# A hybrid decoder layer on one core: a new order for its mixing stage, products k by k between the stages, and both ends rewritten

## The chip, the cores and the metric

The kernel runs on one core of a Trainium2 chip. The metric is the device time of one execution in microseconds (us), the median of the runs shown. TensorE (PE) does the matmuls, VectorE (DVE), ScalarE (ACT) and GpSimd (POOL) the elementwise work, SyncE (SP) issues most of the transfers; each engine works through its own queue in order.

## The reference

512 tokens of 1024 channels in float32 go through a feed-forward layer, a mixing layer of two head groups, and a second feed-forward layer. Each of the three is normed ahead of and behind, and added to x:

```python
def reference(x, ...):
    h = rms_norm(x, ffn1_pre_g)
    x = x + 0.5 * rms_norm(swiglu(h, ffn1_w_in, ffn1_w_out), ffn1_post_g)
    h = rms_norm(x, mix_pre_g)
    q, k, v, u = split(h @ w_mix_in)            # 4 x 512 columns
    attn = dilated_attention(q, k, v)           # 8 heads of 64, causal, with a linear bias
    ssm = s5_mixer(u, ...)                      # 32 groups of 16 channels, 64 complex states each
    mixed = concat([attn, ssm]) @ w_mix_out
    x = x + rms_norm(mixed, mix_post_g)
    h = rms_norm(x, ffn2_pre_g)
    return x + 0.5 * rms_norm(swiglu(h, ffn2_w_in, ffn2_w_out), ffn2_post_g)
```

swiglu is silu(h W1) * (h W2) through 2816 hidden channels. s5_mixer runs a linear recurrence over the tokens, adds a skip term to its output, takes gelu of the sum y, and returns y * sigmoid(y w_glu + b_glu).

## The kernel before

Activations lie with channels on the 128 partitions and tokens along the free axis: a tile holds 8 slices k of 128 channels and 512 tokens. Every operand of a product is split into a high part in a reduced float format and a low part that holds the rest, and `mm3` (L123) multiplies high by high, high by low and low by high into one PSUM bank; so a product over 8 slices is 24 matmuls. A weight is loaded to a tile wraw (3 buffers), ACT casts it to whi and DVE or POOL subtracts for wlo (4 buffers each); `load` (L97) does all of that, and `load_tail` (L104) the same into tiles tw that hold the weights of a product's last slices.

`start` loads x and the first weights in pieces, with SP issuing all transfers, among them smalls (gains and the first weight slice, into sw); PE does six warm-up products idle<-warm meanwhile, and then the products first over k = 0 to 7. `ffn` does the first feed-forward layer; its fill work computes the parameters of the state-space model (`ssm_params`, on DVE, ACT and POOL, two of its tiles being gb and cz). `boundary` stands between two stages: it finishes the last product of the stage behind (yt), norms and adds (`prep`, with a DVE product, sum and low part xl and an ACT high part xh for each k), and begins the products first of the next stage (`begin`), in two halves of 256 tokens, h = 0 and 1. The small products st sum squares over partitions, and rp spreads the result back.

`mix` is the mixing stage. Products prj make q and k, prv makes v; U, the input of the recurrence, is written out (ud<-uT) and read back in another layout (um<-ud). The products st<-um make the states of 128 blocks of four tokens, and `scan` then combines the blocks on DVE in a row of short units; `go(n)` records n units of it, `f(n)` n pieces of the products prj and prv, so the code writes out by hand how these interleave. A pair of heads goes through scores (sc), biased maximum (DVE), exponential (ACT), scaling, transposes (pt, copied to ptt), values (pv) and cat, of which ACT writes the high and DVE the low part. Then come ys (the output of the recurrence, with loads w2<-w2d), gelu (tiles ge, zg, zz), gl (the gate), and mo, the output product, whose first four slices come from cat and whose last four are left to the boundary as a tail. The last stage is a feed-forward layer that ends in `finish`: the last product yt by tokens, a sum with y (gather), squares with a sum on ACT, the gain and the final scaling, and the output's transfer, for four blocks b of 128 tokens in two halves d of 512 channels; DVE's order there is written out.

Matmuls, and every instruction passed through `fix`, keep the order in which the program records them on their engine. All others are placed by the scheduler of the tile framework, which moves them ahead or behind by its own estimates and the buffers.

## Time and profile before

| | us |
|---|---|
| runs | 975.64, 972.04, 975.0 |
| median | 975.0 |
| the profiled execution | 973.89 |
| its span, first to last instruction | 972.1 |

The mean granted clock of PE over the span is 0.99 of full speed. The table gives times of whole executions; the rows further down come from the profiled one, with times from the start of its span. The span's stages are: start and first layer to about 378 us, the first boundary to 406, the mixing stage to about 560, the second boundary, and the last layer.

### The profile page before, as it was taken

What the parts mean: (1) busy time and instruction counts of PE and PEld (TensorE: products, weight loads), DVE (VectorE), ACT (ScalarE), POOL (GpSimd) and SP (SyncE); (2) the same over time, 40 slices, a digit from 0 to 9 for tenths busy, and PEclk for the clock granted to TensorE, in tenths of its full rate; (3) what the DMA queues carried; (4) which work ended last, traced back from release to release, by engine and by line L of the source; (5) the groups of instructions that cost most, each with busy time, mean ns of one, the idle gap of its engine ahead of it and who ended that gap; (6) DMA issues with size and microseconds to landing.
All of it is one profiled execution on the core that took longest, in us unless ns stands there. A gap on an engine that the chain in (4) does not pass through costs nothing.

```text
span 972.1 us, 12842 instructions
## 1 busy us (share of the span) xinstructions
PE 949.6 (98%) x5072; PEld 793.7 (82%) x5072; DVE 528.9 (54%) x930; ACT 370.9 (38%) x612; POOL 223.3 (23%) x134
## 2 busy tenths in 40 slices
PE   9999999999999999999998899999999999999996
PEld 7888888888888899888766699888888888888885
DVE  7997214553266437667978458554225433544427
ACT  7353324442233234455474444443333222323312
POOL 2322212322143133400010024422122212222300
PEclk9999999999999999999998899999999999999998
DMA  7233334353334240482323420322222322333202
GB/s 255 94 109 114 100 112 142 99 188 103 109 109 136 58 152 24 114 217 87 121 75 97 143 87 2 109 87 87 87 95 101 108 87 87 108 103 128 94 1 87
DMA packets 38029, 102.48 MB, mean 105 GB/s; under 512 B 7600, under 2 KB 10672, under 8 KB 37424
## 3 DMA queue, kind: packets, MB, share of 16 engines
q1 hardware_dynamic: 37104, 98.50, 31.7%
q10 hardware_dynamic: 864, 3.15, 0.9%
q8 instruction: 40, 0.66, 0.3%
q14 instruction: 21, 0.17, 0.1%
HBM read 94.03 MB, written 7.60 MB: 105 GB/s over the span
## 4 chain that ended last, share of the span: by engine, by line
PE 88%; DVE 6%; ACT 2%; DMA 2%; issue 1%; SPq 0%; POOL 0%; DVEq 0%; POOLq 0%; ACTq 0%
PE gu L120 46%; PE yo L120 20%; PE yt L120 6%; PE first L120 3%; PE prj L120 3%; PE prv L120 2%; PE mo L120 1%; PE st L120 1%; PE gl L120 1%; DVE xl L143 1%; DVE x L302 1%; PE pv L120 1%; PE pt L819 1%; DVE Hs L1085 1%; DMA wraw<-wmot 1%
## 5 line engine op out<-in xcount | busy, mean ns | idle before, releaser
L93 ACT CAST whi<-wraw 128x1024 fp32r<-128x1024 f32 (+5 forms) x157 | 155.3, 991 | 314.5 <-PE gu L120 129.2
L95 POOL TENSOR_TENSOR wlo<-wraw,whi 128x1024 fp32r<-128x1024 f32 (+2 forms) x62 | 155.9, 2515 | 519.3 <-ACT whi L93 519.3
L120 PE MATMUL gu<-xh,whi 128*128 128x512 f32 x656 | 257.6, 393 | 0.0
L120 PE MATMUL gu<-xh,wlo 128*128 128x512 f32 x656 | 255.6, 390 | 0.0
L120 PE MATMUL gu<-xl,whi 128*128 128x512 f32 x656 | 255.2, 389 | 0.0
L95 DVE TENSOR_TENSOR wlo<-wraw,whi 128x1024 fp32r<-128x1024 f32 (+5 forms) x95 | 111.0, 1172 | 117.9 <-ACT whi L93 117.3
L120 PEld LDWEIGHTS gu<-xh,wlo 128*128 128x128 f32 x656 | 123.1, 188 | 26.1
L120 PEld LDWEIGHTS gu<-xh,whi 128*128 128x128 f32 x656 | 123.2, 188 | 25.1 <-issue 0.4
L120 PEld LDWEIGHTS gu<-xl,whi 128*128 128x128 f32 x656 | 123.2, 188 | 24.9
L404 DVE TENSOR_TENSOR ut<-gu,rs 128x512 f32<-128x512 f32 x41 | 28.3, 689 | 105.1 <-PE gu L120 105.0
L140 DVE TENSOR_TENSOR al<-ut,ah 128x512 fp32r<-128x512 f32 x44 | 70.4, 1603 | 24.9 <-ACT ah L139 24.8
L402 DVE TENSOR_TENSOR gt<-gu,rs 128x512 f32<-128x512 f32 x41 | 28.2, 688 | 51.8 <-PE gu L120 51.6
L120 PE MATMUL yo<-ah,whi 128*128 128x512 f32 x144 | 56.0, 389 | 0.0
L120 PE MATMUL yo<-al,whi 128*128 128x512 f32 x144 | 56.0, 389 | 0.0
L120 PE MATMUL yo<-ah,wlo 128*128 128x512 f32 x144 | 56.0, 389 | 0.0
L120 PE MATMUL yo<-whi,ah 128*128 128x512 f32 x144 | 56.0, 389 | 0.0
L120 PE MATMUL yo<-wlo,ah 128*128 128x512 f32 x144 | 56.0, 389 | 0.0
L120 PE MATMUL yo<-whi,al 128*128 128x512 f32 x144 | 56.0, 389 | 0.0
L139 ACT CAST ah<-ut 128x512 fp32r<-128x512 f32 x44 | 27.2, 621 | 54.9 <-DVE ut L405 54.9
L120 PE MATMUL first<-xl,whi 128*128 128x256 f32 (+1 forms) x144 | 43.3, 301 | 2.5 <-DVE xl L143 2.5
L120 PE MATMUL first<-xh,whi 128*128 128x256 f32 (+1 forms) x144 | 43.9, 305 | 1.0 <-ACT xh L142 0.9
L120 PE MATMUL first<-xh,wlo 128*128 128x256 f32 (+1 forms) x144 | 42.4, 295 | 0.0
(195 smaller groups left out, 1421.9 us busy)
## 6 DMA issues: line engine op xcount, KB each, us to landing
wraw<-w2i SPq DMA_DIRECT2D x44, 512.0 KB, 3.4
wraw<-w1i SPq DMA_DIRECT2D x42, 512.0 KB, 3.5
wraw<-w2o SPq DMA_DIRECT2D x18, 512.0 KB, 3.4
wraw<-w1o SPq DMA_DIRECT2D x16, 448.0 KB, 3.4
wraw<-wmi SPq DMA_DIRECT2D x12, 512.0 KB, 3.5
x<-xT SPq DMA_DIRECT2D x8, 256.0 KB, 5.3
w1d<-w1s SPq DMA_DIRECT2D x8, 256.0 KB, 2.9
w2d<-zb SPq DMA_DIRECT2D x2, 1024.0 KB, 4.9
```

Of the source, the lines that this page charges most:

```text
L93: fix(self.nc.scalar.copy(out=hi, in_=raw))
L95: fix(eng.tensor_tensor(out=lo, in0=raw, in1=hi.bitcast(F32), op=ALU.subtract))
L120: i = self.nc.tensor.matmul(*a, **k)
L139: nc.scalar.copy(out=hi, in_=src)
L140: nc.vector.tensor_tensor(out=lo, in0=src, in1=hi.bitcast(F32), op=ALU.subtract)
L143: fix(nc.vector.scalar_tensor_tensor(out=lo, in0=src, scalar=scale, in1=hi.bitcast(F32), op0=ALU.mult, op1=ALU.subtract))
L302: fix(nc.vector.tensor_tensor(out=xk, in0=t, in1=xk, op=ALU.add))
L402: nc.vector.tensor_tensor(out=gt, in0=o[f][0], in1=r, op=ALU.mult)
L404: nc.vector.tensor_tensor(out=ut, in0=o[f][1], in1=r, op=ALU.mult)
L819: self.fix(nc.tensor.transpose(b[i][:, o:o + P], sc[:, c:c + P], self.ident))
L1085: tt = lambda o, x, y, op: self.fix(V.tensor_tensor(out=o, in0=x, in1=y, op=op))
```

## The change

1. Start: smalls is issued by ACT's queue ahead of everything, the warm-up comes first in the program with five products in place of six, and the memsets of gb and cz, as well as the copy to sm, are kept in program order.
2. Boundary: all eight k of the second half are done k by k over the four outputs; the sums of the second half are asked for one k earlier.
3. Mixing: states ahead of the last 12 products prj and of the first transposes; more scan units between pieces; the scores of the last pair split into products and the rest, with the values of the third pair between; the second pair's reciprocal on POOL and scaling on ACT; products mo in another order, six groups in place of five ahead of ys; wgl loaded ahead of ys; gelu as a generator of three steps that are recorded one, two and three products behind ys, all in fixed order; the four tail weights behind all of it, fixed; the factor 0.25 moves from a product on ACT over zg into the last split.
4. End: the last half block of channels is done as two quarters of 256 columns, each with its gather, square, sum, gain, final and transfer.

The number of matmuls stays, apart from the warm-up product and the last half block's split. The core of the diff (the moves in `mix`, where old and new lines stand far apart, are shown by their new lines and the removed ones that matter):

```diff
+        self.sw = self.tmp("sw")[:, :52 + P]
+        nc.scalar.dma_start(out=self.sw, in_=a["smalls"])
+        warm = self.tmp("warm")[:, :HT]
+        nc.vector.memset(warm, 0.0)
+
+        idle = self.bank("idle")
+        for _ in range(5):
+            self.mm(idle[:, :HT], lhsT=warm[:, :P], rhs=warm, start=True, stop=True)
...
-        for n in [HT] * 6:
-            self.mm(idle[:, :n], lhsT=warm[:, :P], rhs=warm[:, :n], start=True, stop=True)
         nc.sync.dma_start(out=self.x(0), in_=xt[:, 0])
-        sw = self.tmp("sw")[:, :52 + P]
-        nc.sync.dma_start(out=sw, in_=self.a["smalls"])
+        sw = self.sw
...
             begin(0, k)
-            if k == 3:
+            if k == 2:
                 post[1][0](late, fix=fx)
-            if k == 5:
+            if k == 4:
                 rr[1] = post[1][1]()
-        for k in range(4):
+        for k in range(KD):
             prep(1, k)
             begin(1, k)
-        pre[0][0](fixp=fx)
-        for k in range(4, KD):
-            prep(1, k)
-        for i in range(len(w)):
-            for k in range(4, KD):
-                begin(1, k, i)
-            if i == 1:
+            if k == 3:
+                pre[0][0](fixp=fx)
+            if k == 6:
                 pre[0][1]()
...
+        gather(3, 2)
+        gain(3, 2)
+        add_sum(3, 2)
+        for i in range(3):
+            final(3, i)
...
-            nc.gpsimd.memset(gb[q], 0.0)
+            self.fix(nc.gpsimd.memset(gb[q], 0.0))
...
+        return lambda: [self.attn_probs(ap, hp, i, order, place[i]) for i in range(2)]
...
+        if hp < 1:
+            nc.vector.reciprocal(out=rd, in_=den)
+        else:
+            nc.gpsimd.tensor_tensor(out=rd, in0=den, in1=self.mone, op=ALU.pow)
+        for t in range(4):
+            so = sc[:, QOFF[t]:QOFF[t + 1]]
+            if hp < 1:
+                nc.vector.tensor_scalar_mul(so, so, rd[:, t:t + 1])
             else:
...
+        def gelu(n4, b):
+
+            fx, t, z = self.fix, self.tmp("ge"), zg[:, n4]
+            fx(nc.scalar.activation(out=t, in_=b, func=AF.Square))
+            fx(nc.vector.scalar_tensor_tensor(out=t, in0=t, scalar=1.0 / 0.044715, in1=b, op0=ALU.add, op1=ALU.mult))
+            yield
+            fx(nc.scalar.activation(out=t, in_=t, func=AF.Tanh, scale=0.044715 * math.sqrt(2.0 / math.pi)))
+            fx(nc.vector.scalar_tensor_tensor(out=z, in0=t, scalar=1.0, in1=b, op0=ALU.add, op1=ALU.mult))
+            yield
+            self.split(zt[:, n4], zt[:, 4 + n4], z, fix=fx)
+            yield
...
-        sc = scores(0)
+        sc = scores(0)()
         vn = ap.tile([P, 4, S], F32, name="vn", tag="vn", bufs=1)
-        f(3)
-        pt = [turn(sc[0]), turn(sc[1])]
+        f(2)
         for n4 in range(0, NP, 4):
             states(n4)
+        f()
+        pt = [turn(sc[0]), turn(sc[1])]
...
+        parts((0, (0, 1)), (1, (0, 1)))
+        go()
+        sc = scores(3)
+        low = values(2, pt)
+        sc = sc()
         go()
         low()
-        out_attn(2, (0, 1))
+        parts((2, (0, 1)), (3, (0, 1)))
         go()
-        for m in range(3):
-            out_attn(m, (2,))
-        pt = [turn(sc[0]), turn(sc[1])]
+        parts((0, (2,)), (1, (2,)))
+        pt = [turn(sc[0])]
         go()
-        out_attn(3, range(3))
+        parts((2, (2,)), (3, (2,)))
+        pt.append(turn(sc[1]))
+        go()
+        out_attn(4, (0, 1))
         low = values(3, pt)
...
+        go(9)
         low()
...
+        parts((4, (2,)), (5, range(3)))
+        parts(*((m, (3,)) for m in range(6)))
...
+        steps = []
+        for n4 in range(6):
+            if n4 < 4:
+                steps.append(gelu(n4, outputs(n4)))
+            for g in reversed(steps[max(0, n4 - 2):]):
+                next(g)
+        for c in range(4):
+            self.load_tail(bdm, a["wmot"], c, False, self.fix)
```

Three places in the engines' queues, before and after. First PE's queue in the second half of the first boundary, at the end of the first output's products and the beginning of the second's (first_2884 and first_2885 are the first two of the four outputs, whi and wlo their weights; the four outputs' names are one lower in the new program). Before:

```order
L120 MATMUL first_2884<-xh_2879,whi_2856 128x256
L120 MATMUL first_2884<-xl_2880,whi_2856 128x256
L120 MATMUL first_2884<-xh_2879,wlo_2857 128x256
L120 MATMUL first_2885<-xh_2879,whi_2862 128x256
L120 MATMUL first_2885<-xl_2880,whi_2862 128x256
L120 MATMUL first_2885<-xh_2879,wlo_2863 128x256
```

After, from the small sum st in the middle of the second half:

```order
L129 MATMUL st_3376<-ones_90,acc_2880 128x2 x2
L129 MATMUL first_2883<-xh_2878,whi_2855 128x256
L129 MATMUL first_2883<-xl_2879,whi_2855 128x256
L129 MATMUL first_2883<-xh_2878,wlo_2856 128x256
L129 MATMUL first_2884<-xh_2878,whi_2861 128x256
L129 MATMUL first_2884<-xl_2879,whi_2861 128x256
L129 MATMUL first_2884<-xh_2878,wlo_2862 128x256
L129 MATMUL first_2885<-xh_2878,whi_2867 128x256
L129 MATMUL first_2885<-xl_2879,whi_2867 128x256
L129 MATMUL first_2885<-xh_2878,wlo_2868 128x256
L129 MATMUL first_2886<-xh_2878,whi_2873 128x256
```

The first three rows of before stand for the last k of the first output, behind which the second output begins its k = 4; in the new program the four outputs follow each other for each k.

Second, SP's queue where U is written out (ud) and read back (um), among the loads of weights for prj (wmi) and prv (wmv). Before:

```order
L892 DMA ud<-uT 128x512 x4
L99 DMA wraw<-wmi 128x1024
L99 DMA wraw<-wmv 128x1024
L894 DMA um<-ud 32x16x128 x4
L99 DMA wraw<-wmv 128x1024 x3
L787 DMA bias<-bias 128x512 x2
```

After:

```order
L108 DMA wraw<-wmi 128x1024
L108 DMA wraw<-wmv 128x1024
L904 DMA ud<-uT 128x512 x4
L108 DMA wraw<-wmv 128x1024 x2
L906 DMA um<-ud 32x16x128 x4
L108 DMA wraw<-wmv 128x1024
L800 DMA bias<-bias 128x512 x2
```

Two loads now stand ahead of the writes of U, and two between these and the reads. In the same queue, further on, the load of the last gain (gt<-glast) has moved from behind the last loads of the mixing stage to a place ahead of the four loads w2<-w2d.

Third, ACT's queue at the gelu: ge are its Square (from the bank ys) and Tanh, zz the high parts for the gate's product, tw the casts of tail weights, zg the scaling by 0.25. Before:

```order
L932 ACTIVATE ge<-ys 128x512
L934 ACTIVATE ge<-ge 128x512
L93 CAST tw<-wraw 128x1024
L139 CAST zz<-zg 128x512
L932 ACTIVATE ge<-ys 128x512
L93 CAST whi<-wraw 128x1024
L937 ACTIVATE zg<-zg 128x512
L934 ACTIVATE ge<-ge 128x512
L932 ACTIVATE ge<-ys 128x512
L93 CAST tw<-wraw 128x1024
L139 CAST zz<-zg 128x512
L934 ACTIVATE ge<-ge 128x512
```

After:

```order
L948 ACTIVATE ge<-ys 128x512 x2
L951 ACTIVATE ge<-ge 128x512
L948 ACTIVATE ge<-ys 128x512
L951 ACTIVATE ge<-ge 128x512
L148 CAST zz<-zg 128x512
L948 ACTIVATE ge<-ys 128x512
L951 ACTIVATE ge<-ge 128x512
L148 CAST zz<-zg 128x512
L951 ACTIVATE ge<-ge 128x512
L148 CAST zz<-zg 128x512 x2
L102 CAST tw<-wraw 128x1024 x4
```

The casts of tail weights have left the gelu's steps and stand behind the last zz, and the products on zg are gone from this queue.

## Rows read from the trace of the kernel before

**Rows 1.** The page's head and busy line: engine, busy us, share, instructions.

```profile
span 972.1 us, 12842 instructions
...
PE 949.6 (98%) x5072; PEld 793.7 (82%) x5072; DVE 528.9 (54%) x930; ACT 370.9 (38%) x612; POOL 223.3 (23%) x134
```

**Rows 2.** PE's waits: engine, line, what released it: us, times, longest.

```profile
PE mo L120 <- ACT cat L973: 3.1, 1, 3.1
PE first L120 <- DVE xl L143: 2.5, 7, 0.6
...
PE sc L120 <- ACT ptt L821: 1.1, 1, 1.1
```

**Rows 3.** Timeline, start: start, us, engine, line, operation [idle before <- releaser].

```profile
1.19 0.42 SPq L221 DMA_DIRECT2D sw<-smalls  x1
...
3.88 1.89 DVE L235 CAST whi<-sw 128x128 fp32r<-128x128 f32 x1 [2.40 <-DMA sw<-smalls]
...
12.19 0.50 PE L120 MATMUL first<-xl,whi 128*128 128x512 f32 x1 [0.28 <-DVE xl L143]
```

**Rows 4.** Window: us, PE, PEld, DVE, ACT, POOL busy, PEclk, DMA share, GB/s.

```profile
11.00:12.00 1.00, 0.77 (x3) 0.19 (x1) 0.80 (x2) 1.00 (x3) 0.00 (x0) 1.00 1.05 398
```

**Rows 5.** Timeline of the first boundary, PE, and DVE's first preparation.

```profile
377.91 0.28 PE L120 MATMUL first<-xh,whi 128*128 128x256 f32 x1
...
383.67 0.50 PE L120 MATMUL st<-ones,acc 128*128 128x2 f32 x4
...
397.88 0.36 PE L120 MATMUL first<-xh,whi 128*128 128x256 f32 x1
...
401.14 0.39 PE L120 MATMUL first<-xl,whi 128*128 128x256 f32 x1 [0.63 <-DVE xl L143]
...
406.24 0.40 PE L120 MATMUL prj<-xh,whi 128*128 128x512 f32 x1
...
388.52 0.87 DVE L300 SCALAR_TENSOR_TENSOR y<-y,gh,rp 128x256 f32<-128x256 f32 x2 [0.96 <-PE rp L120]
```

**Rows 6.** Timeline of PE in the mixing stage, at the edges of mo and gl.

```profile
508.51 0.73 PE L120 MATMUL mo<-cat,whi 128*128 128x512 f32 x2
...
518.44 2.67 PE L819 MATMUL pt<-ident,sc 128*128 128x128 f32 x20
...
542.91 0.74 PE L120 MATMUL gl<-zz,whi 128*128 128x512 f32 x2
...
560.23 0.62 PE L120 MATMUL mo<-cat,whi 128*128 128x512 f32 x2
```

**Rows 7.** The chain that ended last: start, us, engine, tile, line.

```profile
19.08 10.20 PE gu L120 x45
...
431.73 2.18 PE pt L819 x20
...
539.41 1.05 ACT tw L93
```

**Rows 8.** Window in the mixing stage, columns as in rows 4.

```profile
512.00:519.00 7.00, 4.93 (x12) 3.54 (x13) 6.89 (x13) 1.25 (x3) 0.00 (x0) 0.52 0.00 0
```

**Rows 9.** The tile um: its reload's issues (ns each, first and last), and all landings.

```profile
L894 SPq DMA_DIRECT2D um<-ud x4: 340/484/496, 420.3 to 421.8; - x4
...
DMA to landing us min/median/max: 5.3/5.9/9.3
```

**Rows 10.** Timelines of DVE and ACT in the mixing stage.

```profile
533.02 0.65 DVE L1085 TENSOR_TENSOR Hs<-Hs,sx 128x480 f32<-128x480 f32 x1
...
509.05 3.73 ACT L805 ACTIVATE sc<-sc,rd 128x128 f32<-128x128 f32 x8 [0.94 <-POOL rd L799]
...
547.40 0.59 ACT L932 ACTIVATE ge<-ys 128x512 f32<-128x512 f32 x1
```

**Rows 11.** Timeline of DVE at the end: the last gather, the last small sum.

```profile
965.27 0.68 DVE L503 TENSOR_TENSOR y<-yt,y 128x512 f32<-128x512 f32 x1
...
966.81 0.16 DVE L516 SCALAR_TENSOR_TENSOR sums<-sums 128x1 f32<-128x1 f32 x1
```

More of the change, by code (lines that the diff above doesn't have):

```diff
@@ L304, in prep, with begin @@
             self.sq_acc(acc2[:, hs[h]], xk, k == 0, nc.gpsimd)
[L306 to L307 removed]
+        def begin(h, k):
+            for i in range(len(w)):
                 self.mm3(o[i][:, hs[h]], w[i][0][:, k], w[i][1][:, k], xh(k)[:, hs[h]], xl(k)[:, hs[h]],
@@ L499, in product @@
                 th, tl = tail(k)
-                self.mm3(o[b, d], th[:, ts], tl[:, ts], tw(0, k, d), tw(1, k, d), k == 0, k == NT - 1)
-        def gather(b, d):
-            fx(V.tensor_tensor(out=y(b, d), in0=o[b, d], in1=y(b, d), op=ALU.add))
-            fx(nc.scalar.activation(out=self.tmp("sq"), in_=y(b, d), func=AF.Square, accum_out=sums[:, b, d:d + 1]))
-        def gain(b, d):
-            yg[b, d] = self.wp.tile([P, S], F32, name="yg", tag="whi", bufs=4)
-            fx(V.tensor_tensor(out=yg[b, d], in0=y(b, d), in1=self.gt[:, d], op=ALU.mult))
@@ new lines, in at, with gather, gain @@
+        def at(t, b, i):
+            d, sl = cols(*parts(b)[i])
+            return t(b, d)[:, sl]
+        def gather(b, i):
+            yi = at(y, b, i)
+            fx(V.tensor_tensor(out=yi, in0=o[b, i], in1=yi, op=ALU.add))
+            fx(nc.scalar.activation(out=self.tmp("sq")[:, :yi.shape[-1]], in_=yi, func=AF.Square,
+                                    accum_out=sums[:, b, i:i + 1]))
+        def gain(b, i):
+            d, sl = cols(*parts(b)[i])
+            yg[b, i] = self.wp.tile([P, S], F32, name="yg", tag="whi", bufs=4)[:, :parts(b)[i][1]]
+            fx(V.tensor_tensor(out=yg[b, i], in0=at(y, b, i), in1=self.gt[:, d, sl], op=ALU.mult))
@@ new lines, in final @@
+        def final(b, i):
+            c, n = parts(b)[i]
+            fx(V.scalar_tensor_tensor(out=yg[b, i], in0=yg[b, i], scalar=rs[:, b:b + 1], in1=at(self.xt, b, i),
+                                      op0=ALU.mult, op1=ALU.add))
+            fx((nc.scalar if i == 1 else nc.sync).dma_start(out=self.a["out"][b * P:(b + 1) * P, c:c + n], in_=yg[b, i]))
+        early = [(b, i) for b in range(2) for i in range(2)]
+        for b, i in early:
+            product(b, i, 0, NT - 1)
+        for b, i in early:
+            product(b, i, NT - 1)
@@ L531, in finish @@
         for b in range(2, 4):
-            for d in range(2):
-                product(b, d)
+            for i in range(len(parts(b))):
+                product(b, i)
         for b in range(4):
-            gather(b, 0)
-            gain(b, 0)
-            half_sum(b)
-            if b:
-                final(b - 1, 0)
-                final(b - 1, 1)
-            gather(b, 1)
-            gain(b, 1)
-            scale(b)
-        for d in range(2):
-            final(3, d)
+            for i in range(2):
+                gather(b, i)
+                gain(b, i)
+                add_sum(b, i)
+                if i == 0 and b:
+                    final(b - 1, 0)
+                    final(b - 1, 1)
@@ L994, in fg, with parts @@
                 go(i)
-        fg(1, 1, 1, 2)
-        sc = scores(1)
+        def parts(*mk):
+            for m, ks in mk:
+                out_attn(m, ks)
+        fg(2, 2, 2, 2)
+        sc = scores(1)()
         fg(1, 1, 1, 1)
```

151 lines of the change are left out of this document (56 added, 95 removed).

## The prediction

> **What bounds the kernel now.** The first thing to read is the page's busy line: TensorE (PE) works 949.6 of the 972.1 us of the span [rows 1]. No work is taken off PE by the change, apart from one of six warm-up products, so what can be won is PE's lost time alone. The list of what PE waited for is the second view; the reader sees few entries there, and three that matter: the products mo, first and sc [rows 2]. That list is too short by itself, because a matmul that runs at half clock counts as busy. So the third view is the times at which PE starts its matmuls, against the undisturbed pitch: 45 matmuls of 512 columns in 10.20 us, 0.227 us each [rows 7]. Read so, PE loses time in five places. At the start it reaches the fourth k late, at 12.19 us [rows 3]. In the boundary between two stages 192 half products stand from 377.91 to 406.24 us; the first 48 of them run to 383.67 without a wait, 0.12 us each [rows 5]. That makes 23.0 of 28.3 us. Between them lie 24 small products; four of them and 38 halves take the 5.10 us behind 401.14, so four cost up to 0.54 and all 24 between 2.2 and 3.2. So 2.1 to 3.1 us are lost, and the second boundary is built the same way. In the mixing stage 15 products mo take from 508.51 to 518.44, 9.9 us for 3.4 us of work: 6.5 lost [rows 6]. The 48 products gl take from 542.91 to 560.23, 17.3 us for 10.9: 6.4 lost [rows 6]. The sc products wait 1.1 us for a bank [rows 2]. Part of the mo and gl loss is the clock: between 512 and 519 us the granted clock is 0.52, the lower of its two levels, 1.2 GHz, behind a stretch in which PE stood still for cat [rows 8]. Last comes the end, where VectorE (DVE) works on alone and then the output transfer [rows 11].
>
> **The start.** smalls leaves SP's queue for ACT's, so each later issue moves up by one slot, 0.42 us [rows 3]; one warm-up product of six goes; and the memsets of gb and cz leave the beginning. The DVE copy whi<-sw took 1.89 us beside them [rows 3] and may be shorter now. But none of this ends last. PE is held at 12.19 us by xl, which hangs on the landed x and w1i, so only the earlier landing counts: between 0 and 0.4. I take 0.4, since the first transfers were issued one by one. The DMA engines are already full where PE waits, with a share of 1.05 between 11 and 12 us [rows 4], which is why 0 stays as an end. The Trainium skill (DMA: Bandwidth & Descriptors, section Issuing engines are not separate DMA queues) says that issuing from a second engine saves only the sequencer's issue time, because the transfers share the same engines; by that rule the term would be 0 while they are full, and the sum 0.4 us longer. No other number rests on this sentence.
>
> **The two boundaries.** The second half of the tokens was done k by k up to k = 3, then output by output, so that the first output needed the last k at once: PE stood at 401.14 for the last xl and still had 38 products and a spread ahead [rows 5]. Now all four outputs take k = 4, then 5, 6, 7. The DVE work is the same: eight preparations from 388.52 to 401.1, 1.57 us each, while PE needs 1.44 for a k. With DVE timed as before, PE begins k = 4 at 397.88 as now [rows 5], needs four times 1.44 and 0.4 for the spread, and ends at 404.0 in place of 406.24: 2.2 us. The sums of the second half are also asked for one k earlier; if all the preparations start one k earlier, nothing is left to wait for and the gain is the whole, 3.1 at most. I take 2.6 for each, 5.2 for both (4.4 to 6.2). The cover is thin: DVE's pace is 0.13 us per k slower than PE's.
>
> **The mixing stage, gains.** The mo, gl and sc losses add up to 6.5 + 6.4 + 1.1 = 14.0 us. Their causes are addressed one by one. The scan starts its last step far later than it must: its last write is at 533.02 [rows 10]. Now more units stand between the pieces, eight DVE scalings and two reciprocals of the second pair go to ACT and POOL, and the splits of the tail weights no longer stand among the scan's last units. ACT stood still before 539.41 for a tail weight that had not landed, with the zz cast queued behind it [rows 7]; these loads are now fixed behind the gelu. In the output product the 12 products of two more mo groups stand ahead of the wait for cat.
>
> **The mixing stage, new losses.** (a) The states now come before 12 products prj (2.7 us) and 20 transposes (2.18 us [rows 7]). They need U, which is reloaded by four transfers issued from 420.3 to 421.8 and landing up to 9.3 us later [rows 9]. Before, PE began the states behind the transposes, at 433.9 (431.73 + 2.18 [rows 7]), after U. 4.9 us earlier is 429.0, and the last transfer of U, if it is the one with 9.3, lands at 431.0: PE waits 2.0. SP's queue does not help: ud is issued behind two loads, then come two more loads and only then um, so the same two loads of 512 KB run ahead of U as before. Ends 0.5 and 4. (b) ACT gets eight scalings of the second pair, 3.73 us by those of the last pairs [rows 10], ahead of vn, which PE needs for pv; 0.5 us (0 to 1). (c) cat of the third pair now stands behind two scalings instead of eight (2.8 us less) and behind 6 more products mo (1.4 less), against a wait of 3.1 in the list [rows 2]. Nothing would be left, but DVE has scan pieces among the last scores, so I put 1.3, and 0.5 for the transposes of the second head behind it (0 to 3 for both). (d) gelu in three steps: after the last ys product ACT does Square, Tanh, zz, Tanh and zz at about 0.6 each [rows 10] and DVE the low part, 3.7 us until k = 2 can be finished, of which PE fills 1.6: 2.1 lost (1 to 3). These are 6.4 us of waits. (e) The clock fell behind the wait for cat. The new waits are shorter, but as many. I take one fall, at 15 products with 0.2 us more each, since half the clock doubles 0.227: 3.0 (0 to 9). Net: 14.0 - 6.4 - 3.0 = 4.6 us won.
>
> **The end.** DVE is the engine that ends last there: between its last gather at 965.27 and the last small sum at 966.81 lies 1.54 us [rows 11]. The last half block is now two quarter blocks, each with its own gather, ACT Square and sum in DVE's fixed order, and DVE waits for ACT twice. Half of the 1.54 scales with columns, so two rounds take about 2.1: 0.6 later, and one more final adds a little, while the last transfer carries half the columns. I put 0.5 lost (0 to 0.9).
>
> **The sum.** 0.4 + 5.2 + 4.6 - 0.5 = 9.7 us. The profiled execution took 973.9 us, 1.1 below the median of 975.0 and inside the runs shown; 973.9 - 9.7 = 964.2.
>
> **Rivals.** First: U lands in time and the shorter waits never lower the clock; then 2.0 and 3.0 come back, 959.2. For it speaks that no fall followed the boundary's waits. Second: the clock falls three times, behind the U wait, cat and gl; 6.0 more, 970.2. Third: the boundaries win nothing, because DVE's 1.57 us per k still ends last; 964.2 + 5.2 = 969.4. Against it: PE's 38 products behind the last xl are plain in the rows. Fourth, slower: SP's queue is in order, and gt<-glast now stands ahead of the four w2d loads that ys needs. Its tile takes the scan's memory, so it cannot start before the scan's last DVE instruction. By my walk PE reaches ys at about 529, and a load of that queue lands 5.3 us behind its issue at best [rows 9]; so a scan that ends before 524 costs nothing, and from there each us is a us of PE. I expect its end at 520 to 523. If it ended as late as now, at 533.7 [rows 10], ys would start near 539, some 10 us late, with a clock fall of 3.0 behind it: 964.2 + 13.0 = 977.2, slower than before by 2. Against it: the scan's pieces have more room, as said under the gains.
>
> **How the numbers follow.** Chances: forecast 0.45 (its own range 961 to 967), first rival 0.25, second 0.15, third 0.10, fourth 0.05. The range must reach the first rival with half of its cover (957) and the second (971). A measurement of this kernel tells 0.5% from no change, so faster means below 970.1: 0.45 + 0.25 + 0.09 of the second + 0.07 of the third = 0.86; slower, above 979.9, needs the fourth with more on top, 0.03; the rest 0.11.
>
> **What would show it.** In the changed kernel's profile: in both boundaries the products first without a wait over 0.5 us and the stage 2 to 3 us shorter; the first st<-um held by um<-ud for about 2 us; no ACT wait for a tail weight before zz; gl with about 2 us of waits; one stretch of half clock in the mixing stage; the last small sum of DVE later behind the last gather than 1.54 us. The prediction is wrong if ys waits for w2d, or if the clock falls in the boundaries.

## The result and the profile after

The changed kernel takes 966.7 us in the median (964.99 to 968.64), the kernel before, run beside it, 972.0 (970.39 to 975.64). The ratio is 0.9939, with a 95% interval of 0.9922 to 0.9956: 5.3 us less, where 9.7 were forecast. The time itself, 966.7 against 964.2, lies nearer than the gain does, because the median of before came down from 975.0 to 972.0 when it was run more often. The profiled execution of the changed kernel took 967.4 us, with a span of 965.6 against 972.1.

The page's head and busy line of the kernel after, to be held against [rows 1]:

```profile
span 965.6 us, 12881 instructions
...
PE 944.0 (98%) x5082; PEld 789.4 (82%) x5082; DVE 523.9 (54%) x924; ACT 372.4 (39%) x618; POOL 228.0 (24%) x136
```

PE is busy 5.6 us less, with ten more instructions in the records. The shorter warm-up makes 1.3 of that (4.21 us for 5.49), a part is the clock, whose granted mean rose from 0.990 to 0.994, and the rest isn't taken apart here.

The spans differ by 6.5 us. From PE's start times at the edges of the stages this is where they went (us; a loss has a minus):

| stretch | before | after | won | forecast |
|---|---|---|---|---|
| start to the first small sum of the first boundary | 369.8 | 368.6 | 1.2 | 0.4 |
| rest of yt ahead of the products first, both boundaries | 32.0 | 31.5 | 0.5 | 0 |
| products first, both boundaries | 56.7 | 51.7 | 5.0 | 5.2 |
| begin of the next stage up to its small sum, both | 6.9 | 8.7 | -1.8 | 0 |
| mixing stage, from there to its last product | 159.4 | 156.9 | 2.5 | 4.6 |
| last product and the end | 31.1 | 32.1 | -1.0 | -0.5 |

These add up to 6.4, within rounding the difference of the spans; the last layer from its small sum to its last product takes 316.3 us in both. The medians differ by 1.2 less than the spans: before's profiled execution was 1.8 above its median, after's 0.7. So 1.2 of the 4.4 that are missing is scatter between executions, and 3.2 are terms that came out otherwise than forecast: the begin of the next stage (1.8) and the mixing stage (2.1) above all, less what the start gave beyond its term.

PE's waits in the kernel after (engine, tile and line, what released it: us, times, longest), for [rows 2]:

```profile
PE pv L129 <- DVE nm L805: 3.3, 1, 3.3
PE st L129 <- DMA um<-ud: 1.9, 1, 1.9
...
PE gl L129 <- ACT zz L148: 0.8, 1, 0.8
...
PE sc L129 <- DVE kT L870: 0.7, 1, 0.7
...
PE gu L129 <- DVE wlo L104: 0.5, 1, 0.5
PE prj L129 <- DVE wlo L104: 0.5, 1, 0.5
```

The wait of mo for cat (3.1) is gone, and in its place stands one of 3.3 of the products pv, for a bank that DVE's maxima (nm) had not freed. The 1.9 for the reload of U was forecast. The two of 0.5, for the low part of a weight, were not: they are the beginning of the two next stages, prj and gu.

The clock in the mixing stage, for [rows 8] (columns: us, busy of PE, PEld, DVE, ACT and POOL, granted clock, DMA share, GB/s); the states, the products pv, and the 48 products gl:

```profile
427.80:436.50 8.70, 8.70 (x63) 8.70 (x64) 1.55 (x2) 4.45 (x14) 0.00 (x0) 0.80 0.46 164
509.40:513.30 3.90, 3.90 (x17) 1.59 (x17) 3.90 (x17) 3.46 (x12) 0.26 (x1) 0.58 0.00 0
544.00:557.00 13.00, 11.55 (x48) 8.72 (x48) 8.85 (x11) 8.61 (x12) 0.00 (x0) 1.00 0.36 125
```

Part of the states and most of pv run at 1.2 GHz, each behind one of the two waits above; gl is at the full 2.4 GHz.

### The profile page after: what moved, and what is told of

The parts are those of the page before. It is cut to its first block, busy times and chain, and to the rows that moved or that the text cites. A ratio compares the mean times of both kernels' runs of the same rounds, so it can differ in the third digit from the quotient of the medians.

```text
span 965.6 us, 12881 instructions
## 1 busy us (share of the span) xinstructions
PE 944.0 (98%) x5082; PEld 789.4 (82%) x5082; DVE 523.9 (54%) x924; ACT 372.4 (39%) x618; POOL 228.0 (24%) x136
## 4 chain that ended last, share of the span: by engine, by line
PE 85%; DVE 6%; ACT 4%; DMA 2%; issue 2%; POOL 1%; SPq 0%; POOLq 0%; ACTq 0%; DVEq 0%
PE gu L129 46%; PE yo L129 20%; PE first L129 6%; PE yt L129 5%; PE prj L129 2%; PE st L129 1%; DVE Hs L1111 1%; PE ys L129 1%; ACT sc L818 1%; DVE sx L1111 1%; DMA um<-ud 1%; ACT sc L807 1%; PE mo L129 1%; ACT whi L102 1%; DVE wlo L104 1%
## 5 line engine op out<-in xcount | busy, mean ns | idle before, releaser
L104 POOL TENSOR_TENSOR wlo<-wraw,whi 128x1024 fp32r<-128x1024 f32 (+2 forms) x62 | 159.0, 2564 | 500.0 <-ACT whi L102 492.5
L104 DVE TENSOR_TENSOR wlo<-wraw,whi 128x1024 fp32r<-128x1024 f32 (+5 forms) x95 | 114.0, 1203 | 122.4 <-ACT whi L102 121.7
L400 DVE TENSOR_TENSOR gt<-gu,rs 128x512 f32<-128x512 f32 x41 | 28.2, 689 | 51.8 <-PE gu L129 51.7
```

Source lines behind the costliest of these rows:

```text
L104: fix(eng.tensor_tensor(out=lo, in0=raw, in1=hi.bitcast(F32), op=ALU.subtract))
L400: nc.vector.tensor_tensor(out=gt, in0=o[f][0], in1=r, op=ALU.mult)
```

## The experiments

Each kernel is the changed kernel with the edit shown. Ratios are to the kernel before, run on the same occasion. Since the whole gain is 0.6%, the verdict on a cause mostly rests on the stretch of the profile that the edit touches; there is one profile of each kernel.

**1. The boundary: is it the spread, or the weight buffer?** In the kernel after, PE begins prj at 402.20 and waits 0.5 for the low part wlo of the next weight. ACT makes that weight's high part whi (the cast), DVE the low part. Timelines of the end of the first boundary, kernel after (start, us, engine, line, operation, idle before and what ended it):

```profile
400.82 0.37 ACT L200 COPY rs<-rp 128x256 f32<-128x256 f32 x1 [3.17 <-PE rp L129]
401.09 2.94 ACT L102 CAST whi<-wraw 128x1024 fp32r<-128x1024 f32 x3
402.18 3.50 DVE L104 TENSOR_TENSOR wlo<-wraw,whi 128x1024 fp32r<-128x1024 f32 x3 [4.24 <-ACT whi L102]
402.20 0.50 PE L129 MATMUL prj<-xh,whi 128*128 128x512 f32 x1
403.46 0.50 PE L129 MATMUL prj<-xh,wlo 128*128 128x512 f32 x1 [0.53 <-DVE wlo L104]
```

The cast stands in ACT's queue behind the copy of rp, the spread that PE makes at k = 6. But the cast also needs a free weight buffer, and now that all four outputs go k by k, each weight is in use up to k = 7. The first run asks for the spread one k earlier:

```diff
-            if k == 6:
+            if k == 5:
                 pre[0][1]()
```

> The changed kernel; in both boundaries the spread rp of the norm stands one k earlier (ahead of k = 6 in place of ahead of k = 7). It tells why the first prj waits 0.5 us for wlo. Theory A (ACT's queue: the cast whi stands behind the copy of rp): cast and low part come over 1 us earlier, no wait, first prj to the next small sum 2.8 us in place of 3.6, and the same in the second boundary; 1.6 to 1.8 us faster. Theory B (the weight buffer: whi of the next weights takes the buffer of the first of the four outputs, which now all end with k = 7): the cast still starts at 1.1 us ahead of the first prj, the wait stays at 0.5 and nothing is won. A small new wait of PE for the norm itself (up to 0.4 us each) is possible under both.

The ratio was 0.9956 (0.9938 to 0.9974). ACT in this kernel:

```profile
399.55 0.37 ACT L200 COPY rs<-rp 128x256 f32<-128x256 f32 x1 [1.87 <-PE rp L129]
...
401.23 2.94 ACT L102 CAST whi<-wraw 128x1024 fp32r<-128x1024 f32 x3 [1.30 <-PE first L129]
...
403.59 0.50 PE L129 MATMUL prj<-xh,wlo 128*128 128x512 f32 x1 [0.53 <-DVE wlo L104]
```

The copy is 1.3 us earlier, the cast isn't: ACT stands still for 1.30 until PE has done with a weight. From the first prj to its small sum PE takes 3.66 (3.63 after, 2.75 before). So the buffer binds too, at the same place in time. The second run lets it go earlier, by doing the last two k output by output, the first output first:

```diff
-            begin(1, k)
+            if k < 6:
+                begin(1, k)
...
+        for i in range(len(w)):
+            for k in (6, 7):
+                begin(1, k, i)
+            if i == 0:
+                pre[0][1]()
```

> The changed kernel; in both boundaries k = 6 and 7 of the second half are done output by output, and the spread stands behind the first output. Its xl for k = 7 is there 0.8 us before PE begins k = 6 (397.9 against 398.7), so nothing new should wait. Theory B (weight buffer): the first output ends 2.2 us earlier, its buffer comes free, the cast starts about 2.0 us ahead of the first prj and the wait goes; 0.9 us per boundary, 1.8 in all. Theory A (ACT's queue) gives the same here, since the spread is earlier too. If neither holds, and DVE itself is late, the wait stays.

The ratio was 0.996 (0.9939 to 0.9981). In the second boundary the wait is gone, and gu to its small sum takes 4.11, as before the change, against 5.03 after. In the first boundary only 0.2 came back. ACT at the two places, second boundary ahead:

```profile
609.30 1.05 ACT L102 CAST whi<-wraw 128x1024 fp32r<-128x1024 f32 x1 [1.88 <-PE first L129]
610.25 0.37 ACT L200 COPY rs<-rp 128x256 f32<-128x256 f32 x1
...
400.55 0.37 ACT L200 COPY rs<-rp 128x256 f32<-128x256 f32 x1 [2.42 <-PE rp L129]
400.81 1.05 ACT L102 CAST whi<-wraw 128x1024 fp32r<-128x1024 f32 x1
```

The scheduler put the cast ahead of the copy in one boundary and behind it in the other. Where it is ahead, the freed buffer is used at once; where it is behind, the copy holds it. So there are two causes, one behind the other, and each of the two runs takes only one away. The first kernel of experiment 6 goes at both.

**2. The states behind the first 36 products prj.** The change puts the states ahead of 12 products prj and 20 transposes, and PE then waits for U. This run puts only the 12 products back in front:

```diff
-        f(2)
+        f(3)
         for n4 in range(0, NP, 4):
             states(n4)
-        f()
```

> The changed kernel with the states behind the 12 products prj that the change had put behind them (still ahead of the transposes). Theory: the wait of 1.9 us for um<-ud goes, and with it the fall of the clock behind it (granted 0.80 over the states, 8.8 us for 7.1): 3.8 us faster up to the end of the states, the scan begins earlier, and nothing behind gets later. Rival: ACT copies the states late there, since the exponentials of the first pair stand ahead, and PE waits for a bank instead; then under 2 us are won.

The ratio was 0.9918 (0.9903 to 0.9933), 963.9 us in the median. From the small sum to the transposes PE takes 29.73 where it took 33.57, 3.84 less: 1.9 of the wait, 1.7 of the clock behind it (from the first state's start to the last one's end 7.31 us in place of 9.01), and 0.2 at the edges. Windows of this kernel, the states and gl:

```profile
428.80:435.90 7.10, 7.10 (x66) 7.10 (x65) 2.79 (x3) 5.27 (x15) 0.00 (x0) 1.00 0.71 262
...
539.70:554.60 14.90, 13.46 (x49) 10.08 (x49) 10.31 (x12) 9.99 (x14) 0.06 (x1) 0.89 0.44 140
```

The states are at full clock. But gl, which this edit doesn't touch, now lost part of its clock (0.89) and took 14.9 against 13.3. So of the 3.8 the span kept 3.0. By the ratios the kernel is 2.0 us faster than the changed one, with intervals that overlap.

**3. The scores of the last pair.** Why does pv wait 3.3? DVE, PE and ACT in the kernel after, around the last pair (kT feeds the scores sc; DVE's custom operation takes the maxima nm and frees the bank; POOL takes the reciprocal rd; ACT scales by it; PE transposes the scaled scores):

```profile
498.82 1.23 DVE L104 TENSOR_TENSOR wlo<-wraw,whi 128x1024 fp32r<-128x1024 f32 x1 [3.79 <-ACT whi L102]
...
502.93 0.68 DVE L870 TENSOR_TENSOR kT<-prj,rs 128x512 f32<-128x512 f32 x1
...
503.67 2.43 PE L129 MATMUL sc<-kT,qT 64*128 64x512 f32 x16 [0.68 <-DVE kT L870]
...
508.64 0.69 DVE L805 CUSTOM_DVE_ANT_0 sc<-sc,bias 128x512 f32<-128x512 f32 x1
...
509.39 3.94 PE L129 MATMUL pv<-ptt,vn 128*64 128x512 f32 x16 [3.29 <-DVE nm L805]
...
517.72 1.01 POOL L812 TENSOR_TENSOR rd<-den,mone 128x4 f32<-128x4 f32 x1 [3.67 <-ACT sc L807]
...
518.76 1.92 ACT L818 ACTIVATE sc<-sc,rd 128x128 f32<-128x128 f32 x4 [1.18 <-POOL rd L812]
```

Two things make DVE late. It stood 3.79 us ahead of 498.82, at a split of the first output weight, whose cast ACT had not made, with scan steps and kT queued behind. And between kT and the first maximum it did 5.1 us of other work, steps of the scan and another split. One run moves the scan unit behind the values of the third pair:

```diff
         parts((0, (0, 1)), (1, (0, 1)))
-        go()
         sc = scores(3)
...
         low()
+        go()
         parts((2, (0, 1)), (3, (0, 1)))
```

> The changed kernel; the unit of the scan that stood ahead of the last pair's scores stands behind DVE's maxima and the low part of cat. It asks for the cause of PE's wait of 3.3 us for pv of the third pair, whose bank comes free when DVE takes the first maximum of the last pair's scores (508.64). Theory: DVE does one unit of the scan (about 2.5 us) less ahead of the maximum, so pv starts 2.5 us earlier, and with a wait under 1 us the clock does not fall over pv (3.9 us for 2.3): up to 4 us from the products sc to the next transposes; later, low parts of cat and the scan's end by the same unit, without a wait of PE's over 0.7. Rival: the low part of a weight at the head of DVE's queue (idle 3.8 us before 498.82, for a cast on ACT) is what makes all of it late; then kT still comes at 502.9 and at least 0.8 us of wait is left.

The ratio was 0.9964 (0.9946 to 0.9982). pv starts at 507.67, 1.7 earlier, its wait is 1.6 and there is no clock fall over it (2.3 us for 3.9). From sc to the first transposes PE takes 12.6 against 13.9. But the scan ends later, and that is what the fourth rival of the prediction was about. PE at pv, SP's queue and PE at ys in this kernel:

```profile
507.67 2.37 PE L129 MATMUL pv<-ptt,vn 128*64 128x512 f32 x16 [1.59 <-DVE nm L805]
...
524.51 0.33 SPq L474 DMA_DIRECT2D gt<-glast  x1
525.01 2.64 SPq L125 DMA_DIRECT2D w<-w2d  x4
...
533.15 0.64 PE L129 MATMUL ys<-Hs,w 128*32 128x128 f32 x16 [2.11 <-issue]
```

gt, which takes the scan's memory, goes out when the scan ends, and w2d right behind it. The landings of w2d came 7.9 to 10.0 us after the issue, and ys stood 2.1 us. What the profile calls issue stands ahead of the first product that reads w, and its end fits the first of these landings (525.01 and 7.9). So the 2.3 us won ahead of ys were given back. But the place in the queue alone doesn't explain the wait. In the kernel after, w2d went out later still, released by pv and not by the scan:

```profile
526.07 2.56 SPq L125 DMA_DIRECT2D w<-w2d  x4
```

It landed 4.9 to 7.6 us after the issue there, and PE came to ys at 532.91 and found it. In this run PE came at 530.62. So an earlier arrival of PE and longer landings make the wait together, and why the landings are longer isn't shown (gt's 512 KB landed at about 528.8, while w2d was on its way).

The other run fixes the split behind the last kT:

```diff
-                wm[m // 2] = self.load(a["wmoa"][m // 2], (8, P))
+                wm[m // 2] = self.load(a["wmoa"][m // 2], (8, P), fix=self.fix if m == 0 else lambda i: i)
...
-        fg(2, 1, 1, 1)
+        fg(2, 1, 1)
+        f()
+        need(0)
+        go()
```

> The changed kernel; the split of the first output weight (wmoa) stands in fixed order behind the last kT, so that it no longer blocks the head of DVE's queue ahead of scan units. Theory (the rival of the run before): DVE's 3.8 us of idle time before 498.82 are filled with scan units, kT comes about 4 us earlier (at about 498.5 in place of 502.9), the wait of sc for kT (0.7) goes, and the first maximum comes 2 to 3 us earlier, so PE's wait for pv is about 0.5 us in place of 3.3; 4 to 5 us in all with the clock. If the order of the units alone makes the wait, kT comes earlier, but pv stays at 3 us behind the scores.

kT came 4.2 us earlier, and pv waited 0.3 instead of 3.3:

```profile
498.71 0.69 DVE L870 TENSOR_TENSOR kT<-prj,rs 128x512 f32<-128x512 f32 x1
...
506.31 2.38 PE L129 MATMUL pv<-ptt,vn 128*64 128x512 f32 x16 [0.33 <-DVE nm L805]
```

Yet the ratio was 0.9969 (0.9948 to 0.9991), no better than that of the changed kernel. PE's longest wait is now further on:

```profile
PE pt L831 <- ACT sc L818: 3.0, 3, 2.5
```

And behind it, in the timelines of POOL and ACT:

```profile
514.60 4.89 POOL L812 TENSOR_TENSOR rd<-den,mone 128x4 f32<-128x4 f32 x1 [3.67 <-ACT sc L807]
...
519.52 1.92 ACT L818 ACTIVATE sc<-sc,rd 128x128 f32<-128x128 f32 x4 [5.06 <-POOL rd L812]
```

The transposes wait for ACT's scaling and that for POOL's reciprocal of 128x4 numbers, which took 4.89 us where it took 1.01 in the kernel after. From the reciprocal's start on DVE worked 4.02 us without a break (columns as above):

```profile
514.60:518.62 4.02, 2.88 (x18) 2.17 (x16) 4.02 (x7) 0.00 (x0) 4.02 (x1) 1.00 0.35 120
```

Then came a break of 0.03 us, and the reciprocal ended 0.87 behind it. In the second kernel of experiment 6, with the same fix, DVE's first break came 0.61 us in, and the reciprocal again ended 0.87 behind it, after 1.48. So it seems that DVE held POOL until it paused; no run tests that, and one reciprocal of the kernel after (at 513.04) took 1.01 without a break of DVE in the records.

What the two runs and the others show together: the stretch from sc to the transposes has the length of a chain over other engines, and PE's own waits in it are slack. The chain is maxima on DVE, exponentials on ACT, the reciprocal on POOL, then on ACT two scalings and behind them cat, which the products mo ahead of the transposes read. In the nine kernels that have this part as the kernel after (itself, those of experiments 1, 2, 4 and 5, and the first of 6) ACT begins cat 11.12 us behind the start of sc. Where pv is quick, PE waits for it; in experiment 4:

```profile
514.20 0.50 PE L129 MATMUL mo<-cat,whi 128*128 128x512 f32 x1 [0.70 <-ACT cat L991]
```

In the kernels where the clock fell over pv (after, and both runs of experiment 1) pv takes 3.9 to 4.0 and the 18 products mo behind it 4.2 to 4.3; in those where it didn't (experiment 4, and the last run of experiment 5) they take 2.3 and 5.7. The stretch is 13.7 to 14.0 in both. (In the first kernel of experiment 6 the low clock goes on over mo; the stretch is 15.1 there, and 0.3 of that is left at the next values.) So neither the 3.3 nor that fall of the clock cost what it seems to; DVE's late maxima did.

**4. The last half block in one piece.** The change cuts it into two quarters; this run undoes that:

```diff
-        parts = lambda b: ((0, S), (S, S)) if b < 3 else ((0, S), (S, HT), (S + HT, HT))
+        parts = lambda b: ((0, S), (S, S))
...
-        gather(3, 2)
-        gain(3, 2)
-        add_sum(3, 2)
-        for i in range(3):
+        for i in range(2):
             final(3, i)
```

> The changed kernel with its last half block of output channels done in one piece again. Theory: each of the two rounds costs a fixed share, so the quarters cost 0.9 us behind DVE's first gather and 0.3 us in the last product; from the start of the last product yt to the end of the span 31.1 us in place of 32.1, the whole 1.0 us faster. Rival: the longer end is PE's, the half clock behind the last product; then the stretch stays at 32.1.

DVE at the end, first the kernel after (quarters), to be held against [rows 11], then this run:

```profile
957.95 0.42 DVE L510 TENSOR_TENSOR y<-yt,y 128x256 f32<-128x256 f32 x1
...
960.18 0.16 DVE L525 SCALAR_TENSOR_TENSOR sums<-sums 128x1 f32<-128x1 f32 x1 [0.18 <-ACT sq L511]
...
960.99 1.54 DVE L532 SCALAR_TENSOR_TENSOR yg<-yg,rs,xt 128x512 f32<-128x512 f32 x3 [0.66 <-POOL rs L528]
```

```profile
958.50 0.68 DVE L510 TENSOR_TENSOR y<-yt,y 128x512 f32<-128x512 f32 x1
...
960.04 0.16 DVE L525 SCALAR_TENSOR_TENSOR sums<-sums 128x1 f32<-128x1 f32 x1
```

One round over a half takes 1.70 us from gather to the end of the sum, two over quarters 2.39. From the first product yt of the last block to the end of the span it is 31.29 against 32.11 (before 31.10): the cut costs 0.8. The ratio, 0.995, can't show that, for its interval (0.9932 to 0.9969) is 3.6 us wide. PE's last product ended at 955.75, 2.2 us ahead of the gather of the first quarter, which DVE began without a pause: DVE's own queue sets the end, so columns that are ready earlier win nothing here.

**5. The start.** It won 1.2 where 0.4 was forecast. Three runs undo the late memsets, the issue from ACT, and both:

```diff
-            self.fix(nc.gpsimd.memset(gb[q], 0.0))
+            nc.gpsimd.memset(gb[q], 0.0)
...
-            self.fix(nc.gpsimd.memset(cz[q], 0.0))
+            nc.gpsimd.memset(cz[q], 0.0)
```

> The changed kernel with the memsets of gb and cz free again, so that POOL does them at the beginning. Theory: DVE's copy whi<-sw again takes about 1.9 us beside POOL's memset in place of 0.23, and the first real product starts 1.3 us later (6.4 in place of 5.1); the first sum of the second stage moves by the same 1.3. Rival: only the earlier transfers count, as the prediction had it; then the copy may be long, but the products of the fourth k are as early as now and the start loses under 0.3 us.

```diff
-        nc.scalar.dma_start(out=self.sw, in_=a["smalls"])
...
         sw = self.sw
+        nc.sync.dma_start(out=sw, in_=self.a["smalls"])
```

> The changed kernel with the transfer of smalls in SP's queue again, behind the first of x. Theory: the first product starts as early (the transfer lands within 0.2 us of now), but every later issue is 0.45 us later, and so are the transfers that PE waits for at the third and fourth k; the start loses 0.3 to 0.5 us. Rival: the transfer engines are full, and nothing changes. With the run before, this splits the start's gain of 1.4 us.

> The changed kernel with both undone at once that were undone singly before: smalls in SP's queue and the memsets of gb and cz free. Nine profiles with the new start have the first sum of the boundary between 368.4 and 369.4 us, the kernel before has it at 369.83; each part undone alone left it inside that band (368.78 and 369.07). Theory: the parts cover for each other (a late transfer hides a long copy and the other way round), so with both undone the sum comes at 369.6 to 370.0. Rival: the start's gain comes from neither (the single profile of before is at the late end of a scatter, or the shorter warm-up counts), and the sum stays below 369.4.

The ratios were 0.9943 (0.9921 to 0.9966), 0.9945 (0.9925 to 0.9965) and 0.9961 (0.993 to 0.9993). The start, kernel after, then with the early memsets:

```profile
3.99 0.23 DVE L237 CAST whi<-sw 128x128 fp32r<-128x128 f32 x1 [2.79 <-DMA sw<-smalls]
...
5.08 0.58 PE L129 MATMUL first<-xh,whi 128*128 128x512 f32 x1
```

```profile
2.96 1.80 POOL L706 MEMSET gb<- 128x2048 f32 x1
...
3.68 2.10 DVE L237 CAST whi<-sw 128x128 fp32r<-128x128 f32 x1 [2.48 <-DMA sw<-smalls]
...
4.70 0.99 POOL L736 MEMSET pp<- 128x512 f32 x2
```

Beside POOL's memsets (gb, and cz, which the profile calls pp) the copy takes 2.10 us, alone 0.23, and PE's first product comes 0.84 later. But the small sum comes at 368.78, 0.17 later: the first product isn't what counts. With smalls on SP it comes at 369.07, with both undone at 369.19. In these two PE's late wait [rows 3] is back, at 11.74 and 11.86, where PE is 0.6 and 0.4 us late by its start times; in none of the other kernels with the changed start is it there. The other kernels, with the start as changed, lie between 368.42 and 369.35, and the kernel before at 369.83 in the one profile there is of it. The parts are too small for this scatter: together they are worth some tenths, and how the 1.2 divides between them, the shorter warm-up and chance stays open.

**6. The pieces together.** Three kernels add up what helped. The first has the last half block whole, the states behind prj, the last two k by output with the spread ahead of k = 6:

```diff
             if k == 3:
                 pre[0][0](fixp=fx)
-            if k == 6:
+            if k == 5:
                 pre[0][1]()
+        for i in range(len(w)):
+            for k in (6, 7):
+                begin(1, k, i)
```

> Three repairs of the changed kernel together: the states behind the last 12 products prj, the last two k of each boundary output by output with the spread ahead of them, the last half block whole. Theory: the single gains add up, 3.8 (states) + 1.8 (both boundaries, now that the cast on ACT finds both a free buffer and the copy of the spread done) + 0.8 (end) = 6.4 us below the changed kernel, about 960.3. Rival: the copy of the spread still holds the cast in the first boundary (0.7 less), or the shorter waits come back behind gl as a fall of the clock (2 us less): 961 to 963.

It takes 962.1 us, 0.9903 (0.9887 to 0.9918). Both beginnings wait 0.2 instead of 0.5; prj takes 3.26 to its small sum, gu 4.33: 1.1 of the 1.8 came back, and ACT's cast still stands 0.2 in each until PE has done with a weight. The time is the rival's and not the 960.3 of the theory. The second adds the split behind kT, and holds the loads of the gate's weights behind the gelu as well:

```diff
-        ... (self.load(a["wgl"][m2], (8, P)) for m2 in range(2))
+        ... (self.load(a["wgl"][m2], (8, P), fix=self.fix) for m2 in range(2))
```

> The kernel before it with the first output weight's split fixed behind the last kT, and the gate weights' loads fixed behind the output products. Theory: pv's wait of 3.3 us falls to 0.5 as before, and, since the gate weights no longer take buffers and DVE time among the last scores, POOL's reciprocal takes about 1 us again (4.89 in the run with the split alone) and the last pair's transposes do not wait: 3 to 5 us below the three repairs alone, about 956. Rival: the last pair's way from scores over maxima, exponentials, reciprocal and scaling to the transposes sets the pace there, not the wait for pv; then what PE wins ahead of pv it loses ahead of the transposes pt, and under 1.5 us are won.

962.0 us, 0.9896 (0.9878 to 0.9914), and not 956. PE reaches ys at 526.45, 2.8 earlier than in the first, though it waits 1.1 for U again, and gives it back by a stop of 1.84 within ys and a gl of 14.9 for 13.3. The third adds the scan unit of experiment 3:

> The kernel before it with the scan unit behind DVE's last maxima, too. Theory: no wait for pv at all and maxima another 1 to 2 us earlier, so the last pair's transposes come earlier by that; 1 to 2 us below. Rival: the scan ends later by a unit, the w2<-w2d loads wait behind gt<-glast for it, and ys waits for them (2.3 us in the run with the unit behind the scores alone); then no faster than the kernel before it, or up to 2 us slower.

960.5 us, 0.9891 (0.987 to 0.9911): 11.0 below the kernel before on this occasion, and the lowest ratio of all, though the intervals of the three overlap. From sc to ys PE takes 25.15 where the first takes 29.51 and the kernel after 29.24. There is no wait for w2d here, since the scan now ends before 517.04, when gt goes out. PE's waits in this kernel:

```profile
PE ys L129 <- issue: 1.8, 1, 1.8
...
PE mo L129 <- ACT cat L995: 1.1, 1, 1.1
```

Its stop within ys in PE's timeline, and the window of gl:

```profile
534.79 0.51 PE L129 MATMUL ys<-Hs,w 128*32 128x128 f32 x9 [1.82 <-issue]
...
536.00:551.00 15.00, 13.54 (x50) 10.18 (x50) 10.32 (x12) 10.09 (x14) 0.10 (x1) 0.89 0.41 138
```

So 4.4 us are won over the first up to ys, of which ys takes back 2.2 (12.84 for 10.62) and the clock of gl 1.6.

## Why the prediction was right or wrong

**The products first of the boundaries: right.** 2.5 each for 2.6; PE does 192 halves in 25.83 us, and the thin cover that DVE's pace left held.

**The begin of the next stage: missed.** The prediction costed k by k by the activations alone and took the weights as free. The order decides also when a weight's buffer comes free: for all four at k = 7, and no longer one output after the other. Then the next cast, and the low part behind it, are late: 0.9 each, 1.8 of the 5.0. Experiment 1 shows both the buffer and ACT's queue, and going at both gave 1.1 back.

**The U wait (a): right**, 1.9 for 2.0, and right in its reason, as experiment 2 shows. PE was there at 425.85 and U at 427.78, each 3.2 earlier than said, since the whole stage begins that much earlier. The clock fall behind it, 1.7, was not put there.

**The gelu (d) and gl: right in sum.** gl gained 4.0 for 4.3 (6.4 less 2.1). It takes 13.3, 2.4 above the undisturbed 10.9, of which 0.8 and 0.6 are waits. That the clock stayed up here is luck: in 8 of the 13 profiles of changed kernels gl takes 14.9.

**The scores (b, c): wrong.** Without the clock the prediction had 7.6 won at mo and sc, less 0.5 and 1.8, so 5.3; the profile has 1.5. (From the small sum to ys PE takes 127.1 us for 122.1. That is 5.0 more, where 12 more products mo, 2.8, the wait for U, 1.9, and its clock, 1.7, alone would make 6.4; the difference is the gain, within rounding.) The step that failed is (c): it put 1.3 and 0.5 for scan pieces among the last scores, by walking PE's queue past the wait for cat. DVE's queue was not walked there. In it a split waits at the head for its cast, and a scan unit stands between kT and the maxima. This is 3.8 less than forecast. The third kernel of experiment 6, with both moved and the gate's weights loaded later, wins 4.1 on the kernel after at this place (25.15 for 29.24); ACT begins cat 8.1 us behind the start of sc there and not 11.1.

**The clock: right in kind, wrong in place.** One fall of 3.0 at mo was put in. Two came: 1.7 at the states, and one over pv of 1.6, which cost nothing as the chain sets the length there. So 1.3 came back, and ys gained 0.8 that was not forecast. The mixing stage by these: 4.6 - 3.8 (scores) + 1.3 (clock) + 0.8 (ys) - 0.3 (gl) - 0.1 (the rest) = 2.5. How many falls come is itself chance: the kernels that differ from this one only at the start or the end show none, one, two and three in the same mixing stage.

**The start** was sized at 0.4 and came out at 1.2 in one profile; whether 1.2 or half of it is right stays open. **The end** was sized at 0.5 and cost 1.0, of which the cut has 0.8: with half the columns a gather shrinks from 0.68 only to 0.42, so from the first gather to the last small sum it is 2.23 and not 2.1, the final over three pieces adds 0.1, and 0.2 are lost ahead of the gather. From DVE's last final to the end of the span it is 3.10 us for 3.08, though the last transfer carries half the columns.

**The rivals.** The first (no U wait) and the third (boundaries win nothing) didn't come. The second is near: two falls, one of them without cost. The fourth didn't come in the kernel after, where the scan ended at 523.3 and ys had its weights. In experiment 3 a wait for w2d came, with an end at 524.5. That this lies just beyond the limit of 524 is luck: the limit was made of an arrival of PE at 529 and a landing in 5.3 us, and the run had 530.6 and 7.9, while in the kernel after it wasn't the scan that released w2d.

## What to carry to other kernels

When work is put in another order, walk the queue of each engine that feeds the place, not only that of the engine that waits: at the head of DVE's queue here stood a split that nobody on the path needed yet, and it held everything behind it. An order that gives the products their activations earlier may give back their weight buffers later; price both. And a wait of 3 us on PE may cost nothing where a chain over other engines sets the length of the stretch: compare the whole stretch between two fixed points, with and without the wait, before putting it in a sum.

## What the runs showed of the hardware

**The clock behind a wait is not a fixed price.** Behind a wait for U of 1.1 to 3.2 us the states ran at full clock (7.4 us from first start to last end) in five of ten profiles and lost part of it (8.8 to 9.0) in the other five; without the wait they never did (four profiles, 7.3). The length of the wait doesn't part them: 2.4 us led to no fall, 1.9 to one and to none. gl, which waits 0.8 to 0.9 for its first operand at either clock, took 13.3 us or 14.9. Five kernels have the mixing stage of the kernel after in the same order (itself and those of experiments 4 and 5), and the falls over the states, pv and gl together are 2, 1, 3, 2 and 0 there. Each is a toss of about 1.6 us, a third of what the whole change wins.

**A stop of PE in a long run of small products.** ys is 384 products of 128 columns. In experiment 6 PE stood 1.8 us within it while nothing that the profile shows was late. The transfers of the third kernel there, from 532 to 535 us:

```profile
q8 instruction: 1, 0.02, 2.0%
```

One transfer of 16 KB on the queue for instructions ran from 532.53 to 533.47, and PE went on at 534.79; in the second kernel one ran from 535.64 to 536.63 and PE went on at 538.10; before, from 536.11 to 537.19, with a stop of 0.91 up to 538.62. In the kernel after such a transfer stood there too and the stop was 0.3. In all six profiles with a stop of 0.2 us or more within ys (the wait for w2d aside) PE goes on 1.1 to 1.5 us behind the end of such a transfer; in the other eight the transfers stand there too, and PE doesn't stop. The Trainium skill (Runtime: NRT & Kernel Launch, section Instruction fetch mechanics) says that instructions are fetched in blocks of 16 KiB and that this is mostly hidden. Here the blocks are seen, and stops of up to 1.8 us end at a like distance behind them; that they cause the stops is an inference from the times, and was not tested.

**DVE beside POOL.** A copy of 128x128 takes 0.23 us in the eleven profiles without a memset of POOL beside it. In the three with one it takes 1.89 [rows 3], 1.92 and 2.10. It isn't slowed by a factor there: whenever it starts, between 3.68 and 3.88, it ends at 5.77 or 5.78, 0.1 us behind the end of POOL's last memset. So it is held until POOL is done. The Trainium skill (GPSIMD Engine Reference, section Specifications) says that the two engines share their interfaces to SBUF and names contention with some kinds of DVE instructions. Whether this copy is of such a kind no run shows; that DVE is held while POOL works, the copy's times show. The other way round, POOL's reciprocal of 4.89 us in experiment 3 fits a hold by DVE, as said there, but wasn't tested.
